# Retention scores of 128 queries as joined products, three kinds of work ahead of the filler from the fourth unit on, and two operands of the values asked for later

## The chip, the core and the metric

The kernel runs on one core of one Trainium2 chip. Its engines work at the same time, each through its own queue in order: TensorE (PE) does matmuls, with the loads of its stationary operand shown apart as PEld; VectorE (DVE) and ScalarE (ACT) do elementwise work; SyncE (SP) issues the DMAs. Matmuls write to PSUM, of which this kernel keeps six banks in one pool and two in another; the other tiles lie in SBUF. The metric is the device time of one execution in microseconds (us), lower is better.

## The reference

One encoder block on 1024 tokens of width 1024, all in float32:

```python
h = h + 0.5 * swiglu_ffn(rmsnorm(h, norm_ffn1), ffn1_w_in, ffn1_w_out)
u = rmsnorm(h, norm_mix)
q, k, v, g_ret, p, gates = split(u @ w_in)
q = rotary(q); k = rotary(k) * 256 ** -0.5                 # 4 heads of 256
ret = retention(q, k, v)                                   # below
ret = ret * rsqrt(mean(ret * ret, -1) + eps) * silu(g_ret)
pool_out = multiscale_pool(p, pool_w, pool_scale)
merged = sigmoid(gates[0] + b0) * (ret @ w_ret_up) + sigmoid(gates[1] + b1) * (pool_out @ w_pool_up)
h = h + merged @ w_out
h = h + 0.5 * swiglu_ffn(rmsnorm(h, norm_ffn2), ffn2_w_in, ffn2_w_out)
return rmsnorm(h, norm_final)
```

Retention, written in chunks, keeps a state of 256 x 256 per head:

```python
scores = einsum("bnchd,bnshd->bnhcs", qc, kc) * inner_decay
inner  = einsum("bnhcs,bnshe->bnche", scores, vc)
cross     = einsum("bchd,bhde->bche", q_i * q_decay, state)
new_state = state * chunk_decay + einsum("bchd,bche->bhde", k_i * k_decay, v_i)
out = inner + cross
```

## The kernel before

**Three matmuls for one product.** Every operand is split into a high part (rounded to the matmul's type, on ACT) and a low part (what the rounding left, on DVE). `mm3` (lines 181 to 183) multiplies high by high, high by low and low by high into one PSUM group; each of the three has its own load of the stationary operand. `split` (161, 162) and `split_scaled` (165, 166) make the two parts; `operand`, `weights` and `Next.put` call them.

**The stages.** First feed-forward block; normalisation; the values v; the other projections; retention, with the pooling branch's matmuls as filler; merging; output projection; second feed-forward block. `Flow.run` puts the steps in order: the preparation of a step (loads, splits) is written four steps ahead of its matmuls. Work that isn't tied to a step is put in a list (`flow.add`), of which one or two entries are written after each step; `flow.until` writes entries early when a step needs them. A scheduler then sets each engine's order from what is written, with `soon()` as priority.

**The values.** v = u @ w_v is made in seven products of half-size blocks, in this order: L11 x R11; S2 x T2 and S1 x T1 taken in turn, step by step; S4 x R22 and S3 x T3 in turn; L12 x R21; L22 x T4. Each has four steps of 128 rows, k = 0 to 3. S1 to S4 are sums and differences of weight blocks, made on DVE (`block`), T1 to T4 those of the normalised activations (`Next.t1` to `t4_`, `r21`; in the profile n2R, n2T and bacc). In the profile the weights are vS1w, vS2w and so on, and the PSUM banks vL and vS. Which of the operands goes into the list when is set by `end1`, called with the number of each part that the first feed-forward block's output stage finishes.

**Retention.** Eight units, one for each head and half of the sequence, named 00, 01, 10, ... 31. A unit has two spans s of 256 tokens, each of two blocks j of 128 keys. Its parts, with the names of the profile:
- `scores` (s): for j = 0 the products of 128 keys with 256 queries, for j = 1 with the last 128 queries, for both spans and two halves of the head's width; then scaling by decay (sc) and split (sm).
- `keys` (kd): transposes of k by token on PE (kd00b and so on), scaled and split.
- `update` (st): state products of kd and v, then sf and state on DVE and ACT; `total` carries the sum from span to span. A unit of the first half makes two updates, one of the second half makes one.
- `inner` and `across` (ob): scores by v, and q by the state that was there before.
- `outputs` (o, junk), `normalise` (ir), and `finish`: transposes of both halves (ot), multiplied on DVE by the gate loaded into rg, and stored to ret.

For the last head, `turn` rotates q and k on DVE. The filler is the pooling branch: `px` and `po` make its operands in the first units, `pu0d` to `pu7d` are its up projection, 24 matmuls of 512 columns a step. A unit writes scores, keys, filler, the next unit's loads and values, and the rest (update, inner, across, next unit's operands, outputs).

Of the kernel before, what the change touches and what calls it, by code (L numbers as in the profile page):

```python
# [90 lines left out]
def block_kernel(ctx: ExitStack, tc, x, x_tok, vecs, f1_in, f1_out, w_in, w_v, pool_w, w_ret, w_pool, w_o,  # L91
# [87 lines left out]
    def mm3(dst, w, m, start, stop):  # L179

        mm(dst, w[0], m[0], start=start, stop=False, skip_group_check=True)  # L181
        mm(dst, w[0], m[1], start=False, stop=False, skip_group_check=True)  # L182
        mm(dst, w[1], m[0], start=False, stop=stop, skip_group_check=True)  # L183

    def parts(m, at=slice(None)):
        return m[:, 0, at], m[:, 1, at]
# [924 lines left out]

    mix = Next("n2", V_MIX, h1)

    def end_of(nx):
        def end(part):
            if part == 4:
                nx.work(nx.r21, nx.t4_)
            else:
                nx.work(*{2: (nx.r11,), 5: (nx.r22, nx.p22), 3: (nx.t2, nx.t1, nx.t3)}[part])

        return end

    end1 = end_of(mix)


    tab, stored = {}, set()
# [115 lines left out]
    def values():  # L1242

        nx, kept, two, p1s = mix, {}, {}, {}

        def fetch(r, *rows):

            for z, (k, o) in enumerate(rows):
                load(half(r, z), w_v[k, :, o * H : (o + 1) * H])
            return half(r, 0), half(r, 1)  # L1250

        def rows(n, k):

            if (n, k // 2) not in two:
                at, o = k // 2 * 2 + (4 if n[2] == "2" else 0), (1 if n[1] == "2" else 0)
                two[n, k // 2] = fetch(raw(f"v{n}{k}"), (at, o), (at + 1, o))
            return two[n, k // 2][k % 2]

        def block(n, k):

            if n[0] == "L":
                return rows(n, k)
            if n in ("S1", "S3"):
                return two.pop((n, k))

            L11 = rows("L11", k)
            if n == "S4":
                tt(L11, rows("L12", k), L11, SUB)
                return L11
            L21, L22 = fetch(tl(f"v{n}{k}"), (k, 1), (k + 4, 1))  # L1270
            tt(L22, L21, L22, ADD)
            tt(L21, L11, L21, SUB)
            tt(L11, L22, L11, SUB)
            two["S1", k], two["S3", k] = L22, L21
            return L11

        bk = {}

        def step(L, R, k, where, start, after):
            w = []  # L1280

            def prep():
                t = weights(block(L, k), f"v{L}w{k}")
                w.extend(flat(t, z) for z in range(2))

            def body():
                if start and k == 0:
                    for i in range(4):
                        bk[where, i] = (sum_bank if where == "b" and i < N_SUM else bank)(f"v{L}{i}")
                m = nx.operand(R, k)  # L1290
                for i in range(4):
                    mm3(bk[where, i], parts(m, slice(i * P, (i + 1) * P)), w, start and k == 0, k == 3)
                    if k == 3:
                        with soon():
                            after(i, bk[where, i])

            return prep, body
# [12 lines left out]
        def old(n, i):  # L1310
            return half(kept[n, i // 2], i % 2)

        def result(o, j, other=None):
            def after(i, b):
                c = c2(f"vc{o}{j}{i}")
                if other is None:
                    copy(c, b)
                else:
                    tt(c, b, other(i), ADD)
                flow.add(lambda: store(o, j, i, c))  # L1320
                if (o, j, i) == (0, 0, 3):
                    nx.stats(between=nx.blocks("R22", [("tl", N_TL)] * 3, True))

            return after

        def after1(i, b):
            p1s[i] = c2(f"vp1{i}")
            copy(p1s[i], b)

        def after6(i, b):  # L1330
            copy(keep("h", i), b)

        def after5(i, b):
            copy(keep("f", i), b)

        def product(L, R, where, start, f):
            return [step(L, R, k, where, start, f) for k in range(4)]

        yield from product("L11", "R11", "a", True, after1)
        for p in zip(product("S2", "T2", "a", False, after6), product("S1", "T1", "b", True, after5)):  # L1340
            yield from p
        for p in zip(product("S4", "R22", "b", False, result(0, 1, lambda i: old("h", i))),
                     product("S3", "T3", "a", False, result(1, 1, lambda i: old("f", i)))):
            yield from p
        yield from product("L12", "R21", "b", True, result(0, 0, lambda i: p1s.pop(i)))
        yield from product("L22", "T4", "a", False, result(1, 0))
# [99 lines left out]
    class Unit:  # L1446


        def __init__(self, h, nh):
            self.h, self.nh, self.name = h, nh, f"{h}{nh}"  # L1450

        def loads(self):
            await_stored(f"q{self.h}", f"k{self.h}", f"v{self.name}")
# [58 lines left out]
        def scores(self):  # L1512

            self.sm = []
            for j in range(2):
                wid = SPAN - j * P
                b = bank(f"s{self.name}{j}")
                for s in range(2):
                    at = s * SPAN + j * P
                    for i in range(2):  # L1520
                        mm3(b[:, s * wid : (s + 1) * wid], parts(self.K[i], slice(at, at + P)),
                            parts(self.Q[i], slice(at, at + wid)), s == 0 and i == 0, i == 1)
                n = 2 * wid
                c = c2(f"sc{self.name}{j}")
                m = sb.tile([P, 2, H], F32R, tag="t4", bufs=N_T4, name=f"sm{self.name}{j}")
                with soon():
                    for s in range(2):
                        at = slice(s * wid, (s + 1) * wid)
                        stt(c[:, at], b[:, at], self.row(8, 2 * s + j), self.dec[:, :wid], MUL, MUL)
                    split(m[:, 0, :n], m[:, 1, :n], c[:, :n])  # L1530
                self.sm.append(m)

# [41 lines left out]
        def across(self, s, state):  # L1574
            b, first = self.into(s)
            for t in range(2):
                at = s * SPAN + t * P
                for i in range(2):
                    mm3(self.cell(b, t), parts(self.Q[i], slice(at, at + P)),
                        parts(state, slice(i * HD, (i + 1) * HD)), first and i == 0 and t == 0, i == 1)  # L1580

        def products(self):
            self.ob = {}
            mid = self.update(0)
            if self.nh == 1:
                self.across(0, self.state)
            else:
                self.state = self.update(1)
            for s in range(2):
                self.inner(s)  # L1590
            self.across(1, mid)

        def outputs(self):
            o = self.O[self.nh] = t4(f"o{self.name}")
# [46 lines left out]
    def retention():  # L1641
        filler = fillers()

        def fill(n=1):
            for _ in range(n):
                f = next(filler, None)
                if f is not None:
                    yield f

        yield units[0].operands, units[0].values  # L1650
        for n, u in enumerate(units):
            after = units[n + 1] if n + 1 < len(units) else None

            def scores(u=u, n=n):
                if u.nh == 1:
                    u.follow(units[n - 1])
                u.scores()

            def rest(u=u, after=after):
                u.products()  # L1660
                if after:
                    after.operands()
                u.outputs()
                if u.nh == 1:
                    u.normalise()

            yield none, scores
            yield none, u.keys
            yield from fill()
            if after:  # L1670
                yield after.loads, lambda after=after: (after.values(), after.turn())
            yield none, rest

            late = u.nh == 0 and n
            if n < 3 or late:
                yield from fill()
            if late:
                yield none, units[n - 1].finish
        yield none, lambda: take(range(6))
        yield from fill(2)  # L1680
        yield none, units[-1].finish
        yield none, lambda: take((6, 7))
        yield from fill(2 * KT)
# [278 lines left out]
```

## Time and profile before

| | us |
|---|---|
| median of three runs | 2149.32 (2148.17 to 2150.93) |
| the profiled execution | 2149.24 |
| its span | 2147.2 |
| PE busy | 2134.6 (99%) |
| DVE busy | 1871.7 (87%) |
| ACT busy | 1100.8 (51%) |

The span is the time from the first to the last instruction. Matmuls overlap, so their durations add up to more than they hold PE; what one holds it for is read from the distance of two starts. The values lie at about 590 to 690 us, retention at 1150 to 1330 us.

### The profile page before, as it was taken

To read this page: it belongs to the slowest core of one execution; us is meant where nothing else is said; L and a number is where in the kernel's file an instruction comes from. 1 tells how busy PE (TensorE), PEld (TensorE's weight loads), DVE (VectorE), ACT (ScalarE), POOL (GpSimd) and SP (SyncE) were. 2 spreads that over 40 slices of the span, in tenths; PEclk is the share of its full clock that TensorE was granted. 3 is DMA by queue.
4 is the path that set the end of the run, shared out by engine and by line. 5 is a ranking of instruction groups with operands and counts; after the bars stand their busy time and mean duration, and the time that the engine had idled before them with its cause. 6 is when DMAs were issued, how large, how long until landed. Compare 5 with 4: busy or idle time off the path is not lost.

```text
span 2147.2 us, 30158 instructions
## 1 busy us (share of the span) xinstructions
PE 2134.6 (99%) x10830; PEld 1812.8 (84%) x10830; DVE 1871.7 (87%) x3344; ACT 1100.8 (51%) x2074; POOL 0.2 (0%) x4
## 2 busy tenths in 40 slices
PE   9999999999999999999999999999999999999998
PEld 7888888888887888888888888888888888888887
DVE  8798888997986799999988788899988988899796
ACT  8544444554653544545457653446644544455454
POOL 0000000000000000000000000000000000000000
PEclk9999999999999999999999999999999999999999
DMA  7232323585542333232337566624123232357542
GB/s 257 75 133 74 138 84 134 196 274 177 180 139 89 108 121 114 107 120 108 123 124 231 172 229 235 230 94 161 65 97 124 85 127 84 132 198 274 196 131 100
DMA packets 116102, 313.61 MB, mean 146 GB/s; under 512 B 12784, under 2 KB 17008, under 8 KB 115952
## 3 DMA queue, kind: packets, MB, share of 16 engines
q1 hardware_dynamic: 115376, 310.63, 41.9%
q8 instruction: 85, 1.39, 0.3%
q10 hardware_dynamic: 576, 1.05, 0.1%
q14 instruction: 65, 0.53, 0.1%
HBM read 220.93 MB, written 90.70 MB: 145 GB/s over the span
## 4 chain that ended last, share of the span: by engine, by line
PE 93%; DVE 4%; DMA 1%; ACT 1%; issue 0%; SPq 0%; DVEq 0%; ACTq 0%
PE c_b L181 2%; PE c_b L182 2%; PE c_b L183 2%; PE a_b L181 2%; PE a_b L182 2%; PE a_b L183 2%; PE c_e L181 2%; PE c_e L182 2%; PE c_e L183 2%; PE a_e L182 2%; PE a_e L181 2%; PE a_e L183 2%; PE a_a L181 1%; PE a_a L182 1%; PE a_a L183 1%; PE c_a L182 1%
## 5 line engine op out<-in xcount | busy, mean ns | idle before, releaser
L182 PE MATMUL c_b<-n3T,c_wS 128*128 128x512 f32 x176 | 68.6, 390 | 0.0
L183 PE MATMUL c_b<-n3T,c_wS 128*128 128x512 f32 x176 | 68.5, 389 | 0.0
L181 PE MATMUL c_b<-n3T,c_wS 128*128 128x512 f32 x176 | 68.2, 390 | 0.0
L181 PE MATMUL a_b<-n1T,a_wS 128*128 128x512 f32 x168 | 65.4, 389 | 0.0
L182 PE MATMUL a_b<-n1T,a_wS 128*128 128x512 f32 x168 | 65.4, 389 | 0.0
L183 PE MATMUL a_b<-n1T,a_wS 128*128 128x512 f32 x168 | 65.3, 389 | 0.0
L181 PE MATMUL a_a<-n1R,a_wL 128*128 128x512 f32 x120 | 46.7, 389 | 0.0
L182 PE MATMUL a_a<-n1R,a_wL 128*128 128x512 f32 x120 | 46.7, 389 | 0.0
L183 PE MATMUL a_a<-n1R,a_wL 128*128 128x512 f32 x120 | 46.7, 389 | 0.0
L182 PE MATMUL c_a<-n3R,c_wL 128*128 128x512 f32 x112 | 43.7, 390 | 0.0
L181 PE MATMUL c_a<-n3R,c_wL 128*128 128x512 f32 x112 | 43.6, 389 | 0.0
L183 PE MATMUL c_a<-n3R,c_wL 128*128 128x512 f32 x112 | 43.6, 389 | 0.0
L183 PEld LDWEIGHTS c_b<-n3T,c_wS 128*128 128x128 f32 x176 | 33.0, 188 | 6.9
L181 PEld LDWEIGHTS c_b<-n3T,c_wS 128*128 128x128 f32 x176 | 33.0, 188 | 6.7
L182 PEld LDWEIGHTS c_b<-n3T,c_wS 128*128 128x128 f32 x176 | 33.0, 188 | 6.6
L162 DVE TENSOR_TENSOR a_wS<-a_S,a_wS 128x512 fp32r<-128x512 f32 x45 | 30.6, 682 | 8.2 <-ACT a_wS L161 8.2
L183 PEld LDWEIGHTS a_b<-n1T,a_wS 128*128 128x128 f32 x168 | 31.5, 188 | 6.6
L181 PEld LDWEIGHTS a_b<-n1T,a_wS 128*128 128x128 f32 x168 | 31.5, 188 | 6.5
L182 PEld LDWEIGHTS a_b<-n1T,a_wS 128*128 128x128 f32 x168 | 31.5, 188 | 6.4
L162 DVE TENSOR_TENSOR c_wS<-c_S,c_wS 128x512 fp32r<-128x512 f32 x46 | 31.3, 682 | 3.7 <-ACT c_wS L161 3.6
L182 PE MATMUL c_e<-n3T,c_wL 128*128 128x512 f32 x88 | 34.5, 392 | 0.0
L181 PE MATMUL c_e<-n3T,c_wL 128*128 128x512 f32 x88 | 34.5, 392 | 0.0
(3378 smaller groups left out, 8145.1 us busy)
## 6 DMA issues: line engine op xcount, KB each, us to landing
c_ra<-in_f_in SPq DMA_DIRECT2D x22, 512.0 KB, 3.7
c_rb<-in_f_in SPq DMA_DIRECT2D x22, 512.0 KB, 3.7
a_ra<-in_f_in SPq DMA_DIRECT2D x21, 512.0 KB, 3.7
a_rb<-in_f_in SPq DMA_DIRECT2D x21, 512.0 KB, 3.7
t<-au SPq DMA_DIRECT2D x11, 512.0 KB, 2.9
b<-ag SPq DMA_DIRECT2D x11, 512.0 KB, 4.1
r<-au SPq DMA_DIRECT2D x11, 512.0 KB, 3.7
bra<-in_f_out SPq DMA_DIRECT2D x11, 512.0 KB, 5.5
```

Source lines behind the costliest of these rows:

```text
L162: tt(lo, src, hi.bitcast(F32), SUB)
L181: mm(dst, w[0], m[0], start=start, stop=False, skip_group_check=True)
L182: mm(dst, w[0], m[1], start=False, stop=False, skip_group_check=True)
L183: mm(dst, w[1], m[0], start=False, stop=stop, skip_group_check=True)
```

## The change

Three things, all within what a unit or the values compute; the results are the same sums.

1. In `scores`, for j = 1, a product of three matmuls becomes two: the high part of k by the high and the low part of q side by side (256 columns), and the low part of k by the high part of q (128 columns). The two column blocks are then added: ACT copies the second to SBUF, DVE adds the first from PSUM, and the scaling reads the sum.
2. From the fourth unit (11) on, a unit writes keys, scores and its state updates, all ahead of the filler. Units 00, 01 and 10 keep scores and keys ahead of it and the updates behind. What a unit of the second half takes over from the first (`follow`) is handed over at the end of the first one's rest.
3. R21 and T4 go into the list at the third step (k = 2) of S2 x T2 and S1 x T1, instead of at the end of part 4 of the first feed-forward block.

```diff
-    def end_of(nx):
-        def end(part):
-            if part == 4:
-                nx.work(nx.r21, nx.t4_)
-            else:
-                nx.work(*{2: (nx.r11,), 5: (nx.r22, nx.p22), 3: (nx.t2, nx.t1, nx.t3)}[part])
-
-        return end
-
-    end1 = end_of(mix)
+    def end1(part):
+        mix.work(*{2: (mix.r11,), 5: (mix.r22, mix.p22), 3: (mix.t2, mix.t1, mix.t3)}.get(part, ()))
...
-        for p in zip(product("S2", "T2", "a", False, after6), product("S1", "T1", "b", True, after5)):
+        for k, p in enumerate(zip(product("S2", "T2", "a", False, after6), product("S1", "T1", "b", True, after5))):
+            if k == 2:
+                nx.work(nx.r21, nx.t4_)
             yield from p
...
                 for s in range(2):
-                    at = s * SPAN + j * P
+                    at, to = s * SPAN + j * P, b[:, s * SPAN : (s + 1) * SPAN]
                     for i in range(2):
-                        mm3(b[:, s * wid : (s + 1) * wid], parts(self.K[i], slice(at, at + P)),
-                            parts(self.Q[i], slice(at, at + wid)), s == 0 and i == 0, i == 1)
+                        w, m = parts(self.K[i], slice(at, at + P)), self.Q[i][:, :, at : at + wid]
+                        first, final = s == 0 and i == 0, i == 1
+                        if j == 0:
+                            mm3(to, w, (m[:, 0], m[:, 1]), first, final)
+                        else:
+                            mm(to, w[0], m, start=first, stop=False, skip_group_check=True)
+                            mm(to[:, :P], w[1], m[:, 0], start=False, stop=final, skip_group_check=True)
...
                 with soon():
+                    src = b
+                    if j:
+                        both, src = b.rearrange("p (s z c) -> p s z c", s=2, z=2), c
+                        sums = c[:, :n].rearrange("p (s c) -> p s c", s=2)
+                        copy(sums, both[:, :, 1])
+                        tt(sums, both[:, :, 0], sums, ADD)
                     for s in range(2):
                         at = slice(s * wid, (s + 1) * wid)
-                        stt(c[:, at], b[:, at], self.row(8, 2 * s + j), self.dec[:, :wid], MUL, MUL)
+                        stt(c[:, at], src[:, at], self.row(8, 2 * s + j), self.dec[:, :wid], MUL, MUL)
...
+        def updates(self):
+
+            self.mid = self.update(0)
+            if self.nh == 0:
+                self.state = self.update(1)
+
         def products(self):
             self.ob = {}
-            mid = self.update(0)
+            if self.mid is None:
+                self.updates()
             if self.nh == 1:
                 self.across(0, self.state)
-            else:
-                self.state = self.update(1)
             for s in range(2):
                 self.inner(s)
-            self.across(1, mid)
+            self.across(1, self.mid)
...
                 if u.nh == 1:
                     u.normalise()
-
-            yield none, scores
-            yield none, u.keys
+                else:
+                    after.follow(u)
+
+            if n < 3:
+                yield none, u.scores
+                yield none, u.keys
+            else:
+                yield none, u.keys
+                yield none, u.scores
+                yield none, u.updates
             yield from fill()
```

The instructions' order, at three places. First DVE in the values, while the second weight tile of S1 and S2 is prepared (vS and vL become the weights' sums, n2R are the parts of R21, bacc with `vec` is the step of T4 ahead of its split). Before:

```order
L166 SCALAR_TENSOR_TENSOR n2R_6077<-bacc_4363,vec,n2R_6077 128x512
L166 SCALAR_TENSOR_TENSOR n2R_6080<-bacc_4364,vec,n2R_6080 128x512
L1272 TENSOR_TENSOR vS_6083<-vL_5935,vS_6083 128x512
L166 SCALAR_TENSOR_TENSOR n2R_6104<-bacc_4365,vec,n2R_6104 128x512
L1273 TENSOR_TENSOR vL_5935<-vS_6083,vL_5935 128x512
L166 SCALAR_TENSOR_TENSOR n2R_6107<-bacc_4366,vec,n2R_6107 128x512
L347 SCALAR_TENSOR_TENSOR bacc_4363<-bacc_4363,vec,bacc_4359 128x512
L162 TENSOR_TENSOR vS2w_6089<-vL_5935,vS2w_6089 128x512
L162 TENSOR_TENSOR vS1w_6110<-vS_6083,vS1w_6110 128x512
L162 TENSOR_TENSOR n2T_6134<-bacc_4363,n2T_6134 128x512
```

The second tile's operations stand between those of R21 and T4. After:

```order
L1264 TENSOR_TENSOR vS_6077<-vL_5935,vS_6077 128x512
L1263 TENSOR_TENSOR vS_6121<-vS_6121 128x512
L1265 TENSOR_TENSOR vL_5935<-vS_6077,vL_5935 128x512
L1264 TENSOR_TENSOR vS_6121<-vL_5976,vS_6121 128x512
L166 SCALAR_TENSOR_TENSOR n2R_6142<-bacc_4363,vec,n2R_6142 128x512
L162 TENSOR_TENSOR vS2w_6083<-vL_5935,vS2w_6083 128x512
L162 TENSOR_TENSOR vS1w_6098<-vS_6077,vS1w_6098 128x512
L1265 TENSOR_TENSOR vL_5976<-vS_6121,vL_5976 128x512
L166 SCALAR_TENSOR_TENSOR n2R_6145<-bacc_4364,vec,n2R_6145 128x512
L166 SCALAR_TENSOR_TENSOR n2R_6167<-bacc_4365,vec,n2R_6167 128x512
L162 TENSOR_TENSOR vS2w_6127<-vL_5976,vS2w_6127 128x512
L162 TENSOR_TENSOR vS1w_6148<-vS_6121,vS1w_6148 128x512
```

The second and third tile's differences now stand ahead of the second R21 split, and T4 (L347) begins behind the third tile's weights and the fourth's first operation.

Second PE in unit 11, from the last six matmuls of its scores on (s_11742 is the bank of the 128 queries, kd11b the transposes of the keys, pu1d the filler). Before:

```order
L181 MATMUL s_11742<-q_11627,k_11633 128x128
L182 MATMUL s_11742<-q_11627,k_11633 128x128
L183 MATMUL s_11742<-q_11627,k_11633 128x128
L181 MATMUL s_11742<-q_11630,k_11636 128x128
L182 MATMUL s_11742<-q_11630,k_11636 128x128
L183 MATMUL s_11742<-q_11630,k_11636 128x128
L1434 MATMUL kd11b_11761<-cst,k_11421 128x128 x4
L700 MATMUL pu1d_11771<-po_10991,pu1w_11652 128x512
L701 MATMUL pu1d_11771<-po_10991,pu1w_11652 128x512
```

Behind the 24 filler matmuls come `st` and `ob`. After, with the joined products and the state's products (st) behind them:

```order
L1520 MATMUL s_11746<-q_11621,k_11627 128x256
L1521 MATMUL s_11746<-q_11621,k_11627 128x128
L1520 MATMUL s_11746<-q_11624,k_11630 128x256
L1521 MATMUL s_11746<-q_11624,k_11630 128x128
L181 MATMUL st_11763<-v_11547,kd_11718 128x256
L182 MATMUL st_11763<-v_11547,kd_11718 128x256
L183 MATMUL st_11763<-v_11547,kd_11718 128x256
```

kd11b now stands ahead of the scores, and the filler comes behind the twelve matmuls of `st`, ahead of `ob`.

Third SP's queue around unit 20 (v_11682, q_11684 and k_11687 are its loads, rg the gate of head 0 and ret the store of its result). Before:

```order
L140 DMA v_11682<-v_218 128x1024
L140 DMA q_11684<-q_188 128x512
L140 DMA q_11684<-q_189 128x512
L140 DMA k_11687<-k_196 128x512
L140 DMA k_11687<-k_197 128x512
L140 DMA pu3raw<-in_w_pool 128x1024
L140 DMA pm_236<-pg_11505 128x1024
L140 DMA pg_12446<-gt_231 128x1024
L140 DMA rg_11693<-g_200 128x1024
L140 DMA dec_11690<-in_decay 128x512
L140 DMA rg_11708<-g_201 128x1024
L140 DMA ret_244<-rg_11693 128x1024
```

The loads of unit 20 stand ahead of the gate's. After (the same loads are v_11706, q_11708 and k_11711):

```order
L140 DMA rg_11676<-g_200 128x1024
L140 DMA rg_11691<-g_201 128x1024
L140 DMA v_11706<-v_218 128x1024
L140 DMA pu3raw<-in_w_pool 128x1024
L140 DMA pm_236<-pg_11499 128x1024
L140 DMA ret_244<-rg_11676 128x1024
L140 DMA ret_245<-rg_11691 128x1024
L140 DMA q_11708<-q_188 128x512
L140 DMA q_11708<-q_189 128x512
L140 DMA k_11711<-k_196 128x512
L140 DMA k_11711<-k_197 128x512
```

The gate's two loads come first, and q and k of unit 20 moved behind both stores of ret.

More of the change, by code (lines that the diff above doesn't have):

```diff
@@ L1449, in __init__ @@
         def __init__(self, h, nh):
-            self.h, self.nh, self.name = h, nh, f"{h}{nh}"
+            self.h, self.nh, self.name, self.mid = h, nh, f"{h}{nh}", None
         def loads(self):
@@ L1652, in retention @@
             after = units[n + 1] if n + 1 < len(units) else None
[L1654 to L1657, printed above, removed]
             def rest(u=u, after=after):
```

## The prediction

> **What bounds the kernel now.** I read the page first, then the granted clock, then the chain of waits of TensorE (PE). From the three, word for word:
>
> ```profile
> PE 2134.6 (99%) x10830; PEld 1812.8 (84%) x10830; DVE 1871.7 (87%) x3344; ACT 1100.8 (51%) x2074; POOL 0.2 (0%) x4
> ...
> core 0: 2147.2 us, clock 1.000
> ...
> PE vL L181 <- ACT vS2w L161: 1.5, 1, 1.5
> PE set L204 <- DVE zero L199: 1.2, 1, 1.2
> PE ob L182 <- DVE state L162: 1.1, 2, 0.8
> PE ob L181 <- ACT state L161: 0.6, 2, 0.5
> ```
>
> PE works 99% of the span at full clock, and all its waits of half a microsecond and more are in these four groups (each row ends with total, times, longest). So the time falls only if PE gets fewer or narrower matmuls, or if one of these waits goes; work on other engines counts only where PE comes to wait for it. `set`, at the start, is not touched. The change aims at the matmuls of the scores, at the two `ob` groups and at `vL`. I work against the profiled execution, 2149.24 us with a span of 2147.2 us; the median of the runs shown is 2149.32 us, 0.08 us more.
>
> **Part 1: R21 and T4 asked for later.** The wait of `vL` in the timelines of PE, VectorE (DVE) and ScalarE (ACT); columns are start and duration in us:
>
> ```profile
> 652.83 0.39 PE L182 MATMUL vS<-vS1w,n2T 128*128 128x512 f32 x1
> 653.06 0.39 PE L183 MATMUL vS<-vS1w,n2T 128*128 128x512 f32 x1
> 654.93 0.96 PE L181 MATMUL vL<-vS2w,n2T 128*128 128x512 f32 x3 [1.48 <-ACT vS2w L161]
> ...
> 660.50 0.39 PE L181 MATMUL vL<-vS2w,n2T 128*128 128x512 f32 x1
> ...
> 643.49 1.40 DVE L166 SCALAR_TENSOR_TENSOR n2R<-bacc,vec,n2R 128x512 fp32r<-128x512 f32 x2
> ...
> 647.35 0.74 DVE L347 SCALAR_TENSOR_TENSOR bacc<-bacc,vec,bacc 128x512 f32<-128x512 f32 x1
> ...
> 655.42 0.68 DVE L162 TENSOR_TENSOR vS2w<-vL,vS2w 128x512 fp32r<-128x512 f32 x1
> ...
> 654.26 0.62 ACT L161 CAST vS2w<-vL 128x512 fp32r<-128x512 f32 x1 [1.78 <-DVE vL L1273]
> ```
>
> 512-wide matmuls start 0.23 us apart (652.83 to 653.06), the next one comes 1.87 us after, so 1.64 us are lost. ACT was idle for 1.78 us before it could make vS2w: DVE was late with the difference, since from 643.49 on it made the R21 splits and from 647.35 on the T4 chains between the weights of S2 and S1, and came to this tile's low half at 655.42. R21 and T4 are operands of the last two of the seven products (L12, L22). In the new order on DVE the first R21 split stands four operations later and the two differences of the third weight tile (vS, vL) stand ahead of the other three. Counting 0.6 us for a 512-wide operation by the starts in that stretch (0.66 for one with a scalar), I get the third vS2w's low half at about 650.4, for a need at 654.93 - 1.64 = 653.3. What is late next is the fourth, at about 656.4 for a need at 660.50 - 1.64 = 658.9. So nothing takes the wait's place: **-1.6 us** (between -1.7 and -0.8, the fourth tile then being over 3 us later than I count). No instruction and no DMA is added, and SP's order there is the same.
>
> **Part 2: joined products.** PE at the second half of unit 31's scores (128 queries):
>
> ```profile
> 1304.90 0.28 PE L183 MATMUL s<-q,k 128*128 128x256 f32 x1
> ...
> 1305.02 0.22 PE L181 MATMUL s<-q,k 128*128 128x128 f32 x1
> ...
> 1305.08 0.28 PE L182 MATMUL s<-q,k 128*128 128x128 f32 x1
> 1305.13 0.19 PEld L183 LDWEIGHTS s<-q,k 128*128 128x128 f32 x1
> ...
> 1305.19 0.27 PE L183 MATMUL s<-q,k 128*128 128x128 f32 x1
> 1305.24 0.19 PEld L181 LDWEIGHTS s<-q,k 128*128 128x128 f32 x1
> ...
> 1306.31 0.29 PE L1434 MATMUL kd31b<-cst,k 128*128 128x128 f32 x1
> ```
>
> 256-wide ones start 0.12 us apart. The twelve 128-wide ones take 1306.31 - 1305.02 = 1.29 us, 0.11 each, almost as much as those of twice the width, and the weight loads start 0.11 apart too: here the loads set the pace, not the columns. After the change there are four of 256 columns and four of 128, so eight loads: 0.06 + 7 x 0.112 = 0.85 us at the pace of the loads, 4 x 0.12 + 4 x 0.11 = 0.92 at the pace of each width. I take 0.87: 0.42 us less per unit, **-3.4 us** for eight units (-3.0 to -3.6). The joined form reads two runs of 128 columns from two halves of a tile, and no row of the profile has that. If it took twice the 0.12 us, the eight would need 1.4 us and the part would cost 0.9 us; I take the 256-wide row, as its nearest.
>
> One rule speaks against this part. The Trainium skill ("TensorE: Matmul & The Clock Gate", section "Back-to-back issue gap") gives an isolated gap of N/2.4 + 2.5 ns. An estimate by it: 12 x 56 = 0.67 us before and 4 x 109 + 4 x 56 = 0.66 after, a gain of 0.1 us in all and a sum of -1.8 us. The rows above disagree with it at 128 columns (0.11 us against 0.056), and the same section says that it counts too little at small N in a stream with weight loads.
>
> The new work per unit, and what it resembles:
>
> ```profile
> L588 ACT COPY g3A<-g2x 128x256 f32<-128x256 f32 x2 | 0.7, 373 | 0.2 <-PE g2x L183 0.2
> ...
> L589 DVE TENSOR_TENSOR g3A<-g2x,g3A 128x256 f32<-128x256 f32 x2 | 0.8, 416 | 0.0
> ...
> L1529 DVE SCALAR_TENSOR_TENSOR sc<-s,by,dec 128x128 f32<-128x128 f32 x16 | 4.8, 341 | 0.0
> ```
>
> A copy of 0.37 us on ACT and an addition of 0.42 us on DVE, 3.0 and 3.3 us over eight units; the two scalings of 0.34 us stay. They delay `sm` of the second half by about 0.8 us. Its readers, the last of each group of `ob` products, come behind 24 filler matmuls (24 x 0.23 = 5.5 us), which cover it. Cost on PE: 0, as long as DVE isn't itself late (next part).
>
> **Part 3: keys, scores, states ahead of the filler.** PE where it waits for a state, in units 01, 11 and 21, two rows of DVE in unit 00, and how full the engines are (DVE and ACT in the third and fourth pair of a stretch's row):
>
> ```profile
> 1194.40 0.28 PE L183 MATMUL ob<-v,sm 128*128 128x256 f32 x1
> 1194.84 0.39 PE L181 MATMUL ob<-state,q 128*128 128x256 f32 x1 [0.16 <-ACT state L161]
> 1195.99 0.39 PE L182 MATMUL ob<-state,q 128*128 128x256 f32 x1 [0.77 <-DVE state L162]
> ...
> 1239.39 0.38 PE L181 MATMUL ob<-state,q 128*128 128x256 f32 x1
> 1240.12 0.39 PE L182 MATMUL ob<-state,q 128*128 128x256 f32 x1 [0.34 <-DVE state L162]
> ...
> 1277.86 0.28 PE L183 MATMUL ob<-v,sm 128*128 128x256 f32 x1
> 1278.61 0.39 PE L181 MATMUL ob<-state,q 128*128 128x256 f32 x1 [0.47 <-ACT state L161]
> ...
> 1166.88 1.41 DVE L166 SCALAR_TENSOR_TENSOR po<-px,vec,po 128x512 fp32r<-128x512 f32 x2
> ...
> 1168.20 1.28 DVE L162 TENSOR_TENSOR v<-v,v 128x512 fp32r<-128x512 f32 x2
> ...
> 1160.00:1170.00 10.00, 9.89 (x62) 8.59 (x61) 10.00 (x21) 7.92 (x15) 0.00 (x0) 1.00 0.83 289
> ...
> 1190.00:1200.00 10.00, 9.07 (x64) 8.22 (x63) 10.00 (x18) 8.32 (x21) 0.00 (x0) 1.00 0.72 246
> ...
> 1270.00:1280.00 10.00, 9.53 (x63) 8.45 (x62) 10.00 (x18) 4.61 (x11) 0.00 (x0) 1.00 0.54 186
> ```
>
> Above the usual 0.12 us, unit 01 loses 0.32 + 1.03 us, unit 11 0.61 and unit 21 0.63. The last two belong to the units that get the new order: `st` now ends before the filler, whose 5.5 us are more than the state's DVE work behind it (1.3 us in two operations).
>
> - Unit 11: 0.61 goes. In the new order DVE has three `rg` multiplications (0.6 us each) ahead of the first kd and the two score scalings ahead of the second, where `st` on PE now waits with the filler behind it: I count its kd as ready 0 to 0.5 us late and take 0.35. Net -0.26 us.
> - Units 21 and 30: 0.63 goes. DVE is full in 1270-1280 and has the rotation of both (12 products of halves) in its queue; what is late next is kd and v for `st` of 21 or 30. I take 0.45 us of new wait (0 to 0.8). Net -0.2.
> - Units 10, 20, 31: nothing lost or gained beside part 2. In unit 20 the new order of SP is paid by slack, worked out below.
> - Units 00 and 01 keep their order of parts, but DVE has no idle time there, and the scheduler set its queue anew. In unit 00 the split of v, on which `st` waits, now stands behind two more po (1168.20 - 1166.88 = 1.32 us) and the addition (0.33 by its starts): 1.65 us later, of which I let 1.2 reach PE, as the two po are then done for the filler that follows. In unit 01 the state no longer stands behind v, but behind the low halves of sm, so of the 1.35 us I keep 0.5. Together **+0.35 us** (-1.35 to +1.65).
>
> SP: both loads of `g` for retention head 0 now go out ahead of unit 20's loads, and q and k of unit 20 behind the two stores `ret`, whose buffers they take.
>
> ```profile
> ret<-rg SPq DMA_DIRECT2D x6, 512.0 KB, 3.5
> ...
> k<-k SPq DMA_DIRECT2D x14, 256.0 KB, 3.7
> ...
> 1223.93 1.91 PE L1621 MATMUL ot<-cst,o 128*128 128x128 f32 x16
> ...
> 1241.53 0.28 PE L181 MATMUL s<-q,k 128*128 128x256 f32 x1
> ```
>
> From the start of `ot` (call it T) the four multiplications (0.6 each, a kd of 0.4 between them, from T + 0.5) are done at T + 3.3, the second store has landed at about T + 7.3 with 0.5 of issue, and k, behind q's issue of 0.8, at T + 12; the first reader, the transposes kd20b, stands at about T + 16.9 (17.6 us from `ot` to the scores above, less 0.42 and 0.26). So 5 us are left: cost 0.
>
> **The sum:** -1.6 - 3.4 - 0.26 - 0.2 + 0.35 = -5.1 us; 2149.24 - 5.1 = 2144.1, with the 0.08 us to the median **2144.2 us**, 0.24% less.
>
> **The rivals.**
> - *New waits eat the gain (no change).* For: DVE has no idle time in the three stretches above, and units 00, 01, 21 and 30 lie in or next to them. If the 0.42 us of each new addition reaches PE there (1.7 us) and the two state waits only move elsewhere (0.8 us more than I count), the sum is -2.6: 2146.7 us. Against: DVE catches up in the filler of each unit.
> - *Slower: the state updates wait in front of the filler.* So far 5.5 us of filler stood between kd's transposes and `st`; now `st` reads kd and v at once, and PE, which keeps its order, stands with the filler behind it. Each late microsecond of DVE costs one. It decides when the five units (11, 20, 21, 30, 31) lose over 9.4 us together (5.1 + 4.3), 1.9 each, half of a DVE backlog of six operations: at 2 us each beyond what I count, 2154.2 us. For: DVE full in 1270-1280. Against: kd's transposes stand ahead of the scores there, so kd has the 2.3 us of the scores (12 x 0.12 + 0.87) to get ready.
> - *Joining saves nothing.* The columns stay 12 x 128 = 4 x 256 + 4 x 128 = 1536; if they set PE's time, or the two runs of a joined operand cost as much as a second matmul, the 3.4 us go: -1.7, 2147.6 us. Against: the loads start 0.11 us apart, 256 columns take 0.12. The Trainium skill's section named above gives a gap that follows the columns in this way.
> - *More than forecast:* no wait in 00, 01, 11, 21 at all: -1.6 - 3.6 - 2.6 = -7.8, 2141.5 us.
>
> **How the numbers follow.** 0.2% is 4.3 us (faster below 2145.0, slower above 2153.6), about what a measurement of this kernel can tell from no change. Forecast 0.55, of which 0.08 falls between 2145.0 and 2146; more than forecast 0.09; new waits 0.20; joining saves nothing 0.05; slower by states in front of the filler 0.11. So faster 0.55 - 0.08 + 0.09 = 0.56, no change 0.08 + 0.20 + 0.05 = 0.33, slower 0.11. The predicted time is that of the forecast; its own range is 2142.5 to 2146. The 8-in-10 range leaves out the far end of the gain and the slower case: 2141 to 2150 us.
>
> **What would show it.** In the profile of the changed kernel the `vL` wait is gone and `vS2w` on ACT has no idle time ahead of it; the second half of the scores takes 0.85 to 0.92 us instead of 1.29; no `ob` waits for `state` in units 11 and 21, while small waits of `st` for kd or v appear; in units 00 and 01 waits of 1 to 2 us remain. Wrong would be the forecast if `st` waits stand at over 1 us a unit, if the joined matmuls start 0.2 us apart, or if kd20b waits for k.

## The result and the profile after

The changed kernel takes 2143.47 us in the median (2141.38 to 2145.51 in 8 runs), the kernel before 2149.73 us beside it (8 runs): a ratio of 0.997, 95% interval 0.9959 to 0.9981, so 0.30% less. 2144.2 us were forecast. In a later group of runs the same kernel took 2143.39 us, at 0.9972 (0.9960 to 0.9983).

From the page, the granted clock and the waits of PE, of the changed kernel:

```profile
PE 2129.4 (99%) x10798; PEld 1809.8 (85%) x10798; DVE 1874.5 (88%) x3352; ACT 1104.0 (52%) x2082; POOL 0.2 (0%) x4
...
core 0: 2140.8 us, clock 0.999
...
PE px L181 <- DVE po L166: 1.0, 1, 1.0
...
PE ru1b L183 <- DVE ru1wS L162: 0.3, 1, 0.3
...
PE st L182 <- DVE v L162: 0.2, 1, 0.2
PE s L1520 <- DVE rg L1632: 0.2, 1, 0.2
```

The waits of `vL` and of `ob` for a state are gone. In the changed stages three are new: px for po in unit 00, ru1b for its weights ru1wS in the merge, and unit 31's scores for a PSUM bank that rg (DVE) still reads. That of st for v was there before too, at 0.27 us by the distance of starts, and is 0.37 now. The clock is the same (0.999 against 1.000).

The third step (k = 2) of S2 and S1 in the values, the one that waited, PE and DVE of the changed kernel:

```profile
652.71 0.39 PE L183 MATMUL vS<-vS1w,n2T 128*128 128x512 f32 x1
652.94 0.39 PE L181 MATMUL vL<-vS2w,n2T 128*128 128x512 f32 x1
...
649.29 0.71 DVE L162 TENSOR_TENSOR vS2w<-vL,vS2w 128x512 fp32r<-128x512 f32 x1
```

The step that came 1.87 us after its forerunner now comes 0.23 us after it; the low half whose making began at 655.42 is begun at 649.29. And the second half of a unit's scores, here of unit 11:

```profile
1224.10 0.28 PE L183 MATMUL s<-q,k 128*128 128x256 f32 x1
1224.22 0.28 PE L1520 MATMUL s<-q,k 128*128 128x256 f32 x1
1224.34 0.22 PE L1521 MATMUL s<-q,k 128*128 128x128 f32 x1
1224.40 0.34 PE L1520 MATMUL s<-q,k 128*128 128x256 f32 x1
1224.58 0.23 PE L1521 MATMUL s<-q,k 128*128 128x128 f32 x1
1224.63 0.33 PE L1520 MATMUL s<-q,k 128*128 128x256 f32 x1
...
1225.04 0.22 PE L1521 MATMUL s<-q,k 128*128 128x128 f32 x1
1225.09 0.34 PE L181 MATMUL st<-v,kd 128*128 128x256 f32 x1
```

Eight products take 1225.09 - 1224.22 = 0.87 us, where twelve took 1.29. From the second pair on a pair takes 0.23 us (1224.40 to 1224.63), as much as two loads at the 0.11 us apart that the profile of before showed: the narrow one comes 0.17 or 0.18 us behind the wide one, and the next wide one 0.05 or 0.06 us behind that. The columns are 1536 before and after, so it is not they that the time followed.

Where the time went, by stages. Each number is the gain against the profile of before: the difference of the starts of the first matmul behind the stage, less that difference at its beginning (the units begin with the first product of scores and end with the last `ob`, and the last row ends with the first matmul of the final normalisation; 21, 30 and 31 stand together, since the filler is spread over them in other ways). "Joined and values" is the change without its order.

| us gained | changed | changed again | joined alone | order alone | values alone | joined and values |
|---|---|---|---|---|---|---|
| before the values | 0.39 | -0.21 | -0.03 | -0.15 | 0.50 | -0.16 |
| values | 1.76 | 1.78 | -0.01 | 0.00 | 1.79 | 1.79 |
| projections | 0.23 | 0.22 | 0.07 | 0.07 | 0.25 | 0.25 |
| units 00, 01 | 0.50 | 1.79 | 1.79 | 1.07 | -0.33 | 1.90 |
| unit 10 | 0.43 | 0.43 | 0.43 | 0.00 | 0.00 | 0.43 |
| unit 11 | 0.89 | 0.89 | 0.83 | 0.70 | -0.01 | 0.83 |
| unit 20 | 0.42 | 0.42 | 0.42 | -0.01 | 0.00 | 0.42 |
| units 21, 30, 31 | 1.56 | 1.57 | 0.36 | -0.20 | 0.01 | -1.55 |
| merge, first two groups | -0.45 | -0.88 | -1.03 | -0.47 | 0.23 | 0.23 |
| behind it | 0.66 | -0.13 | 0.68 | 0.58 | 0.53 | 0.97 |

The first and the last row hold no changed code; they show how far executions differ by themselves.

### The profile page after: what moved, and what is told of

The parts are those of the page before. It is cut to its first block, busy times and chain, and to the rows that moved or that the text cites. A ratio compares the mean times of both kernels' runs of the same rounds, so it can differ in the third digit from the quotient of the medians.

```text
span 2140.8 us, 30120 instructions
## 1 busy us (share of the span) xinstructions
PE 2129.4 (99%) x10798; PEld 1809.8 (85%) x10798; DVE 1874.5 (88%) x3352; ACT 1104.0 (52%) x2082; POOL 0.2 (0%) x4
## 3 DMA queue, kind: packets, MB, share of 16 engines
q10 hardware_dynamic: 576, 1.05, 0.1%
## 4 chain that ended last, share of the span: by engine, by line
PE 92%; DVE 5%; DMA 1%; ACT 1%; issue 0%; SPq 0%; ACTq 0%; DVEq 0%
PE c_b L181 2%; PE c_b L182 2%; PE c_b L183 2%; PE a_b L181 2%; PE a_b L182 2%; PE a_b L183 2%; PE c_e L181 2%; PE c_e L182 2%; PE c_e L183 2%; PE a_e L182 2%; PE a_e L181 2%; PE a_e L183 2%; PE a_a L181 1%; PE a_a L182 1%; PE a_a L183 1%; PE c_a L182 1%
```

## The experiments

**Each part alone, and the change without its order.** The first three are the kernel before with one part of the change, the fourth is the changed kernel with the old order in all units:

```diff
-            if n < 3:
+            if n < 8:
                 yield none, u.scores
                 yield none, u.keys
```

Joined products alone: 

> Only the joined products, on the kernel before. If the pace of the weight loads carries the gain (theory): the second half of each unit's scores takes 0.85 to 0.92 us instead of 1.29, eight times 0.42 = 3.4 us on TensorE; the vL wait (1.5) stays; the state waits of units 11 and 21 (0.6 each) stay or move by a few tenths; 2.5 to 3.5 us faster than before. If the waits carry the gain and joining saves nothing (rival): within 1 us of before, the four wide and four narrow products taking 1.2 us or more.

Measured: 2145.86 us, ratio 0.9981 (0.9972 to 0.9991); 4.0 us less than the 2149.91 beside it. That is above the 2.5 to 3.5 us expected, with an interval of 2 us to either side; units 00 and 01 gain 1.79 us in the profile, where the products alone explain 0.84.

Order alone: 

> Only keys, scores and states ahead of the filler from the fourth unit on. Theory: the state waits of units 11 and 21 go (0.61 and 0.63), the vL wait stays, twelve products of 0.11 stay; 0.5 to 1.3 us faster. Rival, the order as carrier of what retention gained: 3 us or more faster. Other rival, new waits of st: no faster or slower, with st waiting for kd or v.

Measured: 2148.65 us, 0.9994 (0.9984 to 1.0003); 1.3 us less, with an interval that holds no change.

R21 and T4 later, alone: 

> Only R21 and T4 asked for later. Theory: the vL wait goes and nothing takes its place, 1.6 to 1.8 us faster, all of it between the start and the end of the values; from there on the trace runs as before. Rival, that DVE work put off meets the projections or retention: under 0.8 us, with new waits behind the values.

Measured: 2148.29 us, 0.9992 (0.9983 to 1.0002); 1.6 us less, with such an interval too; its part shows in the trace.

Without the order: 

> The change without its order: joined products and later R21 and T4, every unit with scores and keys ahead of the filler and states behind it, as before. If the parts add up: as the joined products and the values alone together, 4.5 to 5.2 us faster than before, with state waits in units 11 and 21 of 0.6 each and 1 us slower than the whole change. If the order is what makes the joined products pay (rival): at most 3 us faster, as the waits for state grow by what the products save.

Measured: 2143.86 us, 0.9974 (0.9964 to 0.9985); 6.05 us less. The time is 0.4 us above that of the whole change, where 1 us was expected; its interval holds both.

Waits of PE with the joined products alone, then with the order alone, then with the values alone:

```profile
PE vL L181 <- ACT vS2w L161: 1.5, 1, 1.5
...
PE ru1b L183 <- DVE ru1wS L162: 1.0, 1, 1.0
...
PE ob L182 <- DVE state L162: 0.3, 1, 0.3
```

```profile
PE kd30b L1434 <- DVE k L1483: 0.6, 1, 0.6
```

```profile
PE ob L182 <- DVE state L162: 1.1, 2, 0.8
PE ob L181 <- ACT state L161: 1.0, 2, 0.5
```

With the order alone the waits for states go in units 11 and 21 (in 01 0.30 us is left of 1.35), and kd30b waits for k instead. The values' part is what it was held for: 1.79 us, all in its stage. The joined products give 0.43 and 0.42 us in units 10 and 20, where nothing else differs, so the rival that joining saves nothing falls. The parts add up in time (4.0 + 1.3 + 1.6 = 6.9 against 6.3, with intervals of 2 us to either side each). But the waits for states weren't the order's to take: with the joined products alone units 01, 11 and 21 have none either. In unit 21 the scheduler then puts filler ahead of the products with the state. In unit 11 the state's DVE work stands behind rg, and rg behind its load. DVE there before, without the order, and with the order in unit 31 alone (below):

```profile
1234.40 1.29 DVE L1622 TENSOR_TENSOR rg<-ot,rg 128x512 f32<-128x512 f32 x2 [1.05 <-DMA rg<-g]
```

```profile
1229.45 1.29 DVE L1632 TENSOR_TENSOR rg<-ot,rg 128x512 f32<-128x512 f32 x2 [0.29 <-DMA rg<-g]
```

```profile
1232.52 1.29 DVE L1632 TENSOR_TENSOR rg<-ot,rg 128x512 f32<-128x512 f32 x2 [0.81 <-DMA rg<-g]
```

DVE idles 1.05, 0.29 and 0.81 us for the load, and PE lost 0.61, 0 and 0.36 us at the state: 0.44 or 0.45 us less where it lost anything. Two more profiles agree: 1.04 and 0.61 us with the values alone, 0.33 and 0 with the joined products alone. So the wait in unit 11 goes with a load that came late.

What the order does keep away in the profiles stands in unit 31. Without it, the profiled execution lost most of what the joined products gave from unit 21 on. PE, DVE and ACT there:

```profile
PE ob L181 <- ACT state L161: 1.6, 1, 1.6
...
1310.05 1.29 DVE L162 TENSOR_TENSOR pu6w<-pu6raw,pu6w 128x512 fp32r<-128x512 f32 x2 [4.23 <-ACT pu6w L161]
1311.26 0.68 DVE L1574 SCALAR_TENSOR_TENSOR sf<-sf,st 128x512 f32<-128x512 f32 x1
...
1309.40 1.14 ACT L161 CAST pu6w<-pu6raw 128x512 fp32r<-128x512 f32 x2 [6.26 <-DMA pu6raw<-in_w_pool]
```

The state's work (sf) stands on DVE behind the filler's weights pu6w, and these wait for their load. With states ahead of the filler, sf goes first. Of the 3.1 us between 1.56 and -1.55 in the table, 2.4 are lost at this state (1.77 and 0.61 by the starts) and 0.9 at unit 31's scores, which wait for k; the 0.3 us that the changed kernel loses at rg aren't lost here. This execution took the median time all the same, as it gains 1.2 us behind unit 31.

**The order in the last unit alone.** `n < 7` in place of `n < 3`. 

> The changed kernel with keys, scores and states ahead of the filler in the last unit alone (31). With the joined products alone no unit from 10 to 21 waited for a state; unit 31 did, behind pu6w whose load was late. Theory: the order is worth something in unit 31 only, so this is within 0.5 us of the changed kernel, without state waits in 11 and 21 and without the wait for state in 31. Rival, as forecast: it is worth 0.6 us each in 11 and 21; then these waits are back and this is 1 to 1.3 us slower.

Measured: 2143.15 us, 0.9967 (0.9955 to 0.9980), as fast as the whole change (2143.47, 2143.39). Unit 21 has no wait for a state; unit 11 has the 0.36 us of the late load, and unit 31 waits 0.54 us for k instead. The order from unit 11 to 30 can't be told from nothing in the time, nor can the whole order, by the 2143.86 us without it.

**The order in all units.** `n < 0`. 

> The changed kernel with keys, scores and states ahead of the filler in all eight units. In units 00, 01 and 10 st then stands in front of the filler while DVE has no idle time. By the mechanism that was feared for the later units (states waiting in front of the filler): st waits for kd or v by 1 to 3 us in each of 00 and 01, 1.5 to 4 us slower than the changed kernel. If DVE's priorities keep kd and v early enough: within 0.5 us of it.

Measured: 2147.61 us, 0.9986 (0.9976 to 0.9996), 4.2 us slower than the changed kernel beside it (2143.39). Waits of PE:

```profile
PE st L181 <- ACT kd L165: 1.7, 3, 1.2
PE ru1b L183 <- DVE ru1wS L162: 1.5, 1, 1.5
```

Units 00 and 01 lose 2.56 us against the changed kernel in the same group of runs, unit 10 1.07, and the merge 0.94 more. In units 01 (1.29 and 0.33 us by the starts) and 10 (0.54) `st` waits for kd in front of the filler; in unit 00 it doesn't, there px (0.69) and the scores (0.44) wait. So the forecast's mechanism for a slower kernel exists, in two of the three units tried; from unit 11 on it costs 0.15 and 0.22 us in two places.

**The changed kernel again.** 

> The changed kernel again, beside the kernels of this group. Theory: between 2142 and 2145 us; its profile shows again the waits of unit 00 (px for po about 1.2, st for v 0.4) and no wait for a state in units 01 to 31. If the waits of unit 00 or the late start of unit 31's scores are chance of one execution, they differ here by more than 0.3 us.

Measured: 2143.39 us, as given above. The wait of px in unit 00 shrank from 1.19 us (distance of starts over the usual) to 0.20, so most of it was chance, and not what the theory expected to see again. ACT in the changed kernel's first profile, then in this one:

```profile
1166.16 0.62 ACT L161 CAST pw<-pw 128x512 fp32r<-128x512 f32 x1 [2.36 <-DMA pw<-in_pool_w]
```

```profile
1165.46 0.62 ACT L161 CAST pw<-pw 128x512 fp32r<-128x512 f32 x1 [1.06 <-DMA pw<-in_pool_w]
```

A load of pooling weights landed 5.86 us after its issue instead of 4.57, and po, which frees the bank for px, stands behind its cast on ACT.

**The sums.** Two kernels price them.

```diff
-                        if j == 0:
+                        if j == 0 or self is units[0]:
                             mm3(to, w, (m[:, 0], m[:, 1]), first, final)
```

with the addition left out of unit 00 as well: 

> The changed kernel with the old three products in unit 00 alone, so that no addition enters DVE's full queue there. If the addition and the order that it brings about are what px waits for in unit 00: that loses 0.42 us of joining and gains the 1.9 us of px and st less the 0.3 of before, so 1.2 us faster than the changed kernel, about 2142.3 us, as long as the old wait of 1.35 us in unit 01 doesn't come back; if it comes back, equal. If the wait is of DVE's backlog in any order (rival): 0.4 us slower.

```diff
-                        copy(sums, both[:, :, 1])
-                        tt(sums, both[:, :, 0], sums, ADD)
...
-                        stt(c[:, at], src[:, at], self.row(8, 2 * s + j), self.dec[:, :wid], MUL, MUL)
+                        stt(c[:, at], both[:, s, 0] if j else src[:, at], self.row(8, 2 * s + j), self.dec[:, :wid], MUL, MUL)
```

> The changed kernel without the copy and the addition: the scaling reads the first column block alone, so the product of high k by low q is left out of the scores of 128 queries. It prices the sums. If the filler covers them except in unit 00 (theory): 1 to 2 us faster than the changed kernel, all of it in units 00 and 01. If they cost wherever DVE is full (rival): 2 us or more, spread over 00, 01, 21, 30, 31 with 0.4 each. If they cost nothing at all: the same within 0.5 us.

Measured: 2142.91 us (0.9967, 0.9956 to 0.9979) and 2143.67 us (0.9974, 0.9964 to 0.9984), beside 2143.39 for the changed kernel: neither differs from it. Without the sums retention gains 5.17 us in all, with them 5.10: in these profiles the copies and additions cost 0.07 us at most. 1.3 of the 1.9 us of unit 00 that the first of the two expectations built on were the chance of one execution, and its old form brought 0.70 us of unit 01's wait for a state back. Their profiles lose 2.11 and 3.35 us in the merge:

```profile
PE ru1b L183 <- DVE ru1wS L162: 2.0, 1, 2.0
```

```profile
PE ru1a L181 <- ACT ru1b L481: 1.6, 1, 1.6
PE ru1b L183 <- DVE ru1wS L162: 1.4, 1, 1.4
```

**The merge.** Two kernels were to remove this wait. The first lets GpSimd issue a load:

```diff
-                    load(pair[tile], pm[i + 4 * tile])
+                    nc.gpsimd.dma_start(pair[tile], pm[i + 4 * tile])
```

> The changed kernel with the merge's loads of pm (the pooling branch's results) issued by GpSimd instead of SP, where the load of ru1rb stands behind one of them. Theory: retention now ends sooner and the merge's second group waits for weights (ru1b for ru1wS, 0.5 and 1.0 us in two executions of the changed kernel, 0 before), because ru1rb is issued behind the wait of a pm load on SP; here ru1rb goes out 0.8 to 1.5 us sooner, the ru1b wait falls below 0.3 us, 0.5 to 0.9 us faster than the changed kernel. Rival: DVE's own queue is late in the merge; then the ru1b wait stays at 0.5 to 1 us and the time as well.

Measured: 2144.60 us, 0.9972 (0.9961 to 0.9982); not faster. SP's queue in it:

```profile
1356.38 0.32 SPq L140 DMA_DIRECT2D pm<-pg  x1
1359.02 0.33 SPq L140 DMA_DIRECT2D ru1rb<-in_w_ret  x1
```

ru1rb still goes out 2.6 us behind the store of pm, though no load stands between; that store took 2.6 us to land in the median there. It was not the pm load that held it back, so this theory falls, and with ru1rb in time (DVE has no idle time ahead of it) PE still waited, 1.4 us for ru1wS and 1.3 for ru1a. In the changed kernel DVE did idle for ru1rb, 0.24 us in the first profile and 1.10 in the second.

The distances in all the profiles point further up. From the first transposes of unit 31's result (ot) to the first matmul of ru1b PE takes 42.57 us in every execution without a wait between. From the first multiplication behind those transposes (rg) to the first ru1wS DVE takes 40.1 to 41.9 us in most, with 2.4 to 4.5 us of idle time. The two rows of before:

```profile
1330.90 2.47 DVE L1622 TENSOR_TENSOR rg<-ot,rg 128x512 f32<-128x512 f32 x4
...
1372.21 0.68 DVE L162 TENSOR_TENSOR ru1wS<-ru1S,ru1wS 128x512 fp32r<-128x512 f32 x1
```

By and large the wait grows with the time from ot to rg:

| kernel | ot to rg, us | waits at ru1a and ru1b, us |
|---|---|---|
| joined and values; before; values; joined alone | 0.90; 1.29; 1.46; 1.54 | 0; 0; 0; 1.0 |
| changed; order in 31; changed again; order alone | 2.38; 2.50; 2.53; 2.76 | 0.3; 0.8; 0.8; 0.4 |
| pm by GpSimd; all ahead; old unit 00; no sums; k = 1 | 3.19; 3.73; 3.83; 3.85; 4.00 | 2.7; 1.5; 2.0; 3.0; 2.2 |
| filler's weights by GpSimd | 5.07 | 4.8 |

It isn't the only term: the joined products alone wait 1.0 us though rg comes early, as DVE takes 41.87 us from there to ru1wS. That a late rg makes PE wait is read from these rows and argued; no run moved rg alone.

Before unit 31's end DVE stands ahead of pu6w. Its waits and the landing of pu6raw in the kernel before, then DVE's wait in the changed kernel (second profile):

```profile
DVE pu6w L162 <- ACT pu6w L161: 1.9, 1, 1.9
...
pu6raw<-in_w_pool SPq DMA_DIRECT2D x1, 512.0 KB, 4.2
```

```profile
DVE pu6w L162 <- ACT pu6w L161: 6.1, 1, 6.1
```

The second kernel was to shorten that:

```diff
-                    load(t["raw"][:, : nk * P], src)
+                    nc.gpsimd.dma_start(t["raw"][:, : nk * P], src)
```

> The changed kernel with the loads of the filler's weights (pu0raw to pu7raw) issued by GpSimd instead of SP; DVE's order stays as it is. Theory of the merge's wait: DVE stands 6 to 8 us ahead of pu6w, since pu6raw goes out on SP behind a store of ret and just ahead of six loads of ret, and lands 6.7 us after; what follows on DVE is late by that, up to the multiplications rg behind unit 31's transposes (2.4 to 2.5 us after the first ot, 1.3 before), and from there DVE is full for 40 to 41 us until ru1wS, while TensorE takes 42.57 from ot to ru1b. If so: pu6w's wait falls by 3 us or more, rg follows ot by less than 1.8, the ru1b wait is under 0.3, 0.5 to 1 us faster than the changed kernel. Rival: the rest of DVE's work ahead of rg decides; the wait at pu6w falls, rg's distance and the ru1b wait stay. If GpSimd's issues land later than SP's: pu6w's wait stays or grows and with it the ru1b wait.

Measured: 2146.98 us (2144.64 to 2151.76 in 11 runs), 0.9990 (0.9981 to 0.9999), 3.5 us more than the changed kernel's 2143.47 in another group of runs. Its waits, and the landing of pu6raw in it and in the changed kernel (second profile):

```profile
PE ru1a L181 <- ACT ru1b L481: 1.8, 1, 1.8
PE ru1b L183 <- DVE ru1wS L162: 1.7, 1, 1.7
PE ru1a L181 <- ACT ru1wL L161: 1.3, 1, 1.3
...
DVE pu6w L162 <- ACT pu6w L161: 6.7, 2, 6.3
...
pu6raw<-in_w_pool POOLq DMA_DIRECT2D x1, 512.0 KB, 6.9
```

```profile
pu6raw<-in_w_pool SPq DMA_DIRECT2D x1, 512.0 KB, 6.7
```

pu6raw is issued no sooner (16.8 us ahead of ot, 16.7 in the changed kernel) and lands no sooner, DVE still waits for it, rg is 5.07 us behind ot, and the merge loses 5.8 us. That SP's queue holds pu6raw back is thus refuted. What the six loads of ret did shows in SP's queue of this kernel, in the changed kernel's (second profile), and on DVE of this one:

```profile
1312.24 3.09 SPq L140 DMA_DIRECT2D ret<-ret  x6
```

```profile
1307.59 4.44 SPq L140 DMA_DIRECT2D ret<-ret  x6
```

```profile
1312.87 0.69 DVE L162 TENSOR_TENSOR pu6w<-pu6raw,pu6w 128x512 fp32r<-128x512 f32 x1 [6.34 <-ACT pu6w L161]
...
1317.09 0.69 DVE L323 TENSOR_TENSOR rut<-ret 128x512 f32<-128x512 f32 x1 [1.17 <-DMA ret<-ret]
```

Here they go out when pu6raw, issued at 1305.27, has landed (1312.2), and it took 6.9 us all the same; without the order it took 7.15 with none of them out. So they don't explain the 6.7 us where it took 4.2 before, and what does stays open. Nor is pu6w what makes rg later here than in the changed kernel: it begins 9.2 us ahead of ot, against 9.4. Behind it DVE waits 0.31 us for pu6w again, 1.13 for ACT's junk and 1.17 for these loads of ret, 2.6 us together against 0.3. Of the 4.9 us that the merge loses beyond the changed kernel's 0.88, 2.5 come before rg and 2.4 between rg and ru1wS.

**R21 and T4 a step sooner.** `if k == 1:` in place of `if k == 2:`. 

> The changed kernel with R21 and T4 asked for one step sooner (k = 1). By counting 0.6 us for each operation of DVE in the new queue, the third tile's difference is ready at about 651.7 and its high half at 652.3 for a need at 653.3, its low half at about 653.5: theory, a wait of 0 to 0.4 us. Rival, that the wait was not DVE's queue but something else that k = 2 moved: the whole 1.6 us stays or goes regardless.

Measured: 2144.70 us, 0.9977 (0.9966 to 0.9987); the values gain 0.49 instead of 1.78 us.

```profile
PE vL L181 <- ACT vS2w L161: 1.0, 1, 1.0
...
659.42 0.62 ACT L161 CAST vS2w<-vL 128x512 fp32r<-128x512 f32 x1 [3.06 <-DVE vL L1265]
```

The third tile is in time, but the fourth isn't, by 1.1 us by the starts: the wait moves with DVE's queue, a tile later than expected.

## Why the prediction was right

The time was right (2144.2 forecast, 2143.47 measured, within the forecast's own range of 2142.5 to 2146), by terms that were right in part and one that was missing. From the values to the merge's first two groups the two profiles gain 5.3 and 6.2 us, where 5.1 were forecast; the remaining 1.05 us of the first and -0.34 of the second lie in code that didn't change.

- *Values, -1.6:* right, with its mechanism. 1.76 and 1.78 us in two profiles, 1.79 alone; the fourth tile's low half was done at 656.2 (655.49 + 0.71), where 656.4 was counted. The sign given for it didn't hold: ACT has 1.93 us of idle time ahead of the third vS2w, which is now so early (648.11) that it doesn't matter.
- *Joined products, -3.4:* right. 0.87 us for eight products was forecast and measured, 0.42 and 0.43 us in the units that show it alone. The Trainium skill's isolated gap ("TensorE: Matmul & The Clock Gate", "Back-to-back issue gap") would have given 0.01 a unit; the rows decided against it.
- *The sums, 0:* right, retention gains 0.07 us more without them.
- *Units 11, 21 and 30, -0.46:* the size was near (0.46 us beyond the products in unit 11, where 0.26 was forecast; with 31, 0.30 where 0.2 was), the cause wrong. "0.61 goes" because `st` ends before the filler: it goes without that too, since the wait in 11 goes with the load of g, and the joined products alone let the scheduler part the one in 21. The `st` waits, counted at 0.35 and 0.45, came out at 0.15 and 0.22 in 11 and 21.
- *Units 00 and 01, +0.35:* wrong in sign but for chance. Of the 1.65 us by which v was to come later in unit 00, 1.2 were to reach PE; `st` waits 0.37 for v, 0.10 more than before, and unit 01's 1.35 went altogether, where 0.5 was to stay. The two units gained 1.79 us, or 0.50 when the load of pw was late; beside the 0.84 of the products that is 0.95 gained, or 0.34 lost as forecast, but by another wait. Why unit 01's wait went altogether stays open: it went with the joined products alone too, and shrank to 0.30 with the order alone.
- *Unit 31, 0:* 0.32 us of wait for rg came in, as the scores now stand behind kd31b and ask for a bank sooner.
- *The merge:* no term of the sum. It gives back 0.45 and 0.88 us: PE comes to ru1b sooner than its weights are ready. In the second profile that takes back 0.88 of the 1.3 us by which 00 and 01 did better than their term; that the two errors have opposite signs is luck, and part of why the time came out so near.

Of the rivals, "new waits eat the gain" came true in a place that was not looked at, and takes up to 0.88 us of 6.3; "states in front of the filler" showed in units 01 and 10 when they were tried, and above 0.22 us there only; "more than forecast" came true in so far as no wait for a state is left in 01, 11 and 21; k of unit 20 was never late.

## What to carry to other kernels

In this kernel, which PE bounds, a matmul of 128 columns with its own weight load took 0.11 us, the pace of the loads, and one of 256 columns 0.12. Joining the two that share a stationary operand saved a load each, and the addition on an engine that the filler covers cost nothing that can be seen. When PE is made faster in a stage that ends in work of another engine and its transfers, look for the next place where PE needs that engine's result, and count that engine's chain from a common start. A wait behind a transfer can be chance: before crediting a change with it, look at what the transfer did in a second profile.

## What was not expected

- The landing of single loads of 256 KB (pw) and 512 KB (g, pu6raw) went with waits of PE three times: pw 1.3 us later, a wait of 1.19 instead of 0.20 us in the same kernel; g, and with it rg's idle time of 0.29, 0.81 and 1.05 us, a wait of 0, 0.36 and 0.61; pu6raw, which landed 4.0 to 7.2 us after its issue, a wait of 1.6 at unit 31's state without the order.
- Of the 3.5 us by which the filler's weights issued from GpSimd were slower, none was in retention itself (5.19 us gained, against 5.10): in the profile it showed about 40 us later, in the merge.
- Executions of unchanged code differ: up to the values by 2.5 us (the kernel with the order in unit 31 alone, slower than before), behind the merge's first two groups by up to 1.7 (0.97 gained without the order, 0.69 lost with the filler's weights by GpSimd). One profile each can't price a part below that; the stage's own distances can, to a tenth.
